# Gates by Tanh with the halves folded into later factors, and the channel norm traced at high priority, in a hybrid decoder layer

## The chip, the cores and the metric

The kernel runs on one core of a Trainium2 chip. A core has a matrix engine (TensorE; PE for its matmuls and PEld for its weight loads in the profile), a vector engine (DVE), an activation engine for pointwise functions (ACT), a general engine (GpSimd; POOL), and a synchronisation engine (SP), which here issues most of the transfers between the chip's memory and the core's own memory (SBUF). TensorE writes its products into a separate memory, PSUM, which DVE and ACT read. Each engine works through its own queue in order and waits at semaphores for the others. The metric is the device time of one execution, in microseconds (us); less is better.

## What is computed

One layer: an input projection `proj = rmsnorm(x) @ w_in` is cut into the inputs of three head groups. Their outputs, side by side, go through `w_out` and are added to `x`, and a last norm follows. All is in 32-bit floating point; x is 512 tokens of 2048 features.

```python
u = cv_a * jax.nn.sigmoid(cv_b)                       # 4 groups of 128 channels
u = causal_depthwise_conv(u, conv_w[l], conv_b[l])    # 31 taps
u = jax.nn.silu(layernorm(u, conv_ln_g[l], conv_ln_b[l]))   # over 512 channels
y_conv = (u @ w_conv_pw[l]) * jax.nn.silu(cv_gate)

y_fox = fox_attention(fq, fk, fv, logf)               # 8 heads, causal, with a forget bias
y_fox = y_fox * jax.nn.silu(fox_gate)

y_mem = memory_attention(mq, mk, mv)                  # 4 heads, into 256 memory tokens
y_mem = y_mem * jax.nn.silu(mem_gate)

x = x + jnp.concatenate([y_conv, y_fox, y_mem], axis=-1) @ w_out[l]
return rmsnorm(x, final_g)
```

## The kernel before

**Operands.** TensorE gets each 32-bit operand as two parts, a rounded high part and the rest. `split` (L90) makes them: a copy on ACT (L93, or L96 with a scale), then a subtraction on DVE (L94, or L97 with a scale). A product is three matmuls: high by high, high by low, low by high. `operand` (L127) does this for a piece of weights that SP has loaded into one of six `raw` buffers; the pair of parts goes into one of three `wb` buffers.

**Projections in pairs.** `pair` (L525) projects two blocks of 128 features at once by seven products in place of eight, with sums of the tokens' quarters made beforehand (`s1` to `s4`). Each product is 24 matmuls at L549. Between products DVE subtracts weight pieces from one another (L511, `raw<-raw,raw`, 128 x 1024) and adds partial results (L508), and ACT copies partial results out of PSUM (L522, L559). A pair hands on its first block as two halves in PSUM (`x1`, `x2`) and its second as a tile `col` in SBUF.

**What runs between.** The list `work` (L971) gives the order of the pairs. Per head of the forgetting attention there is one pair for query and key, one for gate and value (F_G, F_V), and behind heads 0, 2 and 4 one for a group of conv channels. What has to be done with a pair's result is put into `slots`, a queue of small pieces; after each product one piece is taken (`beside`, L513), and from `bg` one convolution tap (L383). `gate_values` (L858) is such a piece: it computes the gate by Silu on ACT out of PSUM in two halves (L862) and transposes the values. `probs` (L888) makes the scores on TensorE, adds the bias and takes the extremum on DVE (L896), the exponential on ACT (L900), the reciprocal of its sum on DVE (L901) and the scaling on ACT (L902). `attend` (L904) transposes the probabilities, multiplies by the values and then by the gate on DVE (L928; L931 for the last head), and POOL's queue stores the result (L929).

**The convolution.** `conv_channels` (L365) computes sigmoid of the gate block (L371) into `up`, multiplies by the other block (L375) and queues 31 taps: the first as an affine on ACT with the bias (L378), the others on DVE (L383). The taps' weights `cwt` come out of a transpose in PSUM (L307). The four results go to the chip's memory and are read back for the norm.

**The channel norm and its product.** The piece `norm` (L953) stands in `slots` behind the attention of head 6. It closes the attention's pool of tiles, loads the four channel groups (`open_norm`, L688, on SP through `queued`), subtracts the mean (`centre`, L696) and divides by the deviation (`normalise`, L706). The sums over channels are matmuls by a constant matrix (L684, L685). The reciprocal root is an exponential of a logarithm on ACT (L717, L718) and one Newton step on DVE (L719 to L721). During this the pairs of the conv gates run (`after_gates`, L725; Silu at L729 and L730), then the pair of query and key of head 7. In the middle of that pair's program order stands `project_conv` (L734): Silu of the normed channels on ACT (L739), the split into `csh` and `csl`, and 48 matmuls of 512 columns.

**Order.** The code is a trace: the program gives dependences and a first order, and a planner at build time sets each engine's final order by simulated times, with earlier traced work first among what is ready. `tc.high_priority()` puts the instructions traced inside it ahead of the others that are ready. `queued` keeps its SP transfers in the order of the program; `issue_after` keeps an instruction behind another on the same engine. Where two functions that follow one another on ACT don't share a table, the build puts a table load (ACT_TABLE_LOAD) ahead of the second.

Of the kernel before, what the change touches and what calls it, by code (L numbers as in the profile page):

```python
# [13 lines left out]
AF = mybir.ActivationFunctionType  # L14
ALU = mybir.AluOpType
# [32 lines left out]
def hybrid_layer_kernel(  # L48
# [18 lines left out]
    nc = tc.nc  # L67
# [12 lines left out]
    def nm(s):  # L80
        uid[0] += 1
        return f"{s}_{uid[0]}"
# [100 lines left out]
    with tc.tile_pool(name="start", bufs=1) as st:  # L183
# [119 lines left out]
        for c in range(CW // P):  # L303
            nc.tensor.transpose(
                pt[:, c * TAPS : (c + 1) * TAPS], cwr[:, c * P : (c + 1) * P], ident[:TAPS, :TAPS]
            )
        nc.vector.tensor_copy(cwt.rearrange("p c j -> p (c j)"), pt)  # L307

    conv_b_c = lambda c: cols[:, 2 * KT + c : 2 * KT + c + 1]
    ln_g_c = lambda c: cols[:, 2 * KT + 4 + c : 2 * KT + 5 + c]  # L310
# [51 lines left out]
    def halves(t):  # L362
        return [t[:, :M], t[:, M:]]

    def conv_channels(c, xs, gate):  # L365

        background(len(bg))
        up = cp.tile([P, PAD + S], F32, tag="up", name=nm("up"))
        acc = cp.tile([P, S], F32, tag="acc", name=nm("acc"))
        nc.gpsimd.memset(up[:, 0:PAD], 0.0)  # L370
        nc.scalar.activation(up[:, PAD:], gate, AF.Sigmoid)  # L371
        w = S // len(xs)
        for i, x_ in enumerate(xs):
            u = up[:, PAD + i * w : PAD + (i + 1) * w]
            nc.vector.tensor_tensor(u, x_, u, ALU.mult)  # L375

        def first():
            nc.scalar.activation(  # L378
                acc, up[:, 0:S], AF.Identity, scale=cwt[:, c, 0:1], bias=conv_b_c(c)
            )  # L380

        def tap(j):
            return lambda: nc.vector.scalar_tensor_tensor(  # L383
                acc, up[:, j : j + S], cwt[:, c, j : j + 1], acc, ALU.mult, ALU.add
            )

        bg.append(first)
        bg.extend(tap(j) for j in range(1, TAPS))
        bg.append(lambda: nc.gpsimd.dma_start(out=accd[c], in_=acc))
# [298 lines left out]
    def open_norm():  # L688
        lp = ln["pool"] = lnpool.enter_context(tc.tile_pool(name="ln", bufs=1, reuse_waits="tile"))
        background(len(bg))  # L690
        acc = ln["acc"] = [lp.tile([P, S], F32, name=f"la{c}") for c in range(NC)]
        for c in range(NC):
            queued(acc[c], accd[c])
        ln["gates"] = [lp.tile([P, S], F32, name=f"lg{c}") for c in range(NC)]

    def centre():  # L696
        acc = ln["acc"]
        total = spare()
        nc.vector.tensor_tensor(total, acc[0], acc[1], ALU.add)
        for c in range(2, NC):  # L700
            nc.vector.tensor_tensor(total, total, acc[c], ALU.add)
        mu = over_channels(total)
        for c in range(NC):
            nc.vector.tensor_tensor(acc[c], acc[c], mu, ALU.subtract)
# [153 lines left out]
    def gate_values(xs, col):  # L858
        fx = fox["pool"]
        gate = fx.tile([P, S], F32, tag="fgate", name=nm("fgate"), bufs=2)  # L860
        for x_, g in zip(xs, halves(gate)):
            nc.scalar.activation(g, x_, AF.Silu)  # L862
        vp = at()
        for j in range(NT):
            sl = slice(j * P, (j + 1) * P)
            nc.tensor.transpose(vp[:, sl], col[:, sl], ident)
        v = tuple(fx.tile([P, NT, P], F32R, tag=t, name=nm(t)) for t in ("vh", "vl"))
        split(*v, vp.rearrange("p (j d) -> p j d", d=P))
        return gate, v
# [34 lines left out]
    def attend(h, gv, pr):  # L904

        pth, ptl = fox["h"], fox["l"]

        def transposes(j):
            n = S - j * P
            tp = at((P, n))  # L910
            for i in range(j, NT):
                nc.tensor.transpose(  # L912
                    tp[:, (i - j) * P : (i - j + 1) * P], pr[i][:, j * P : (j + 1) * P], ident
                )
            w = max(n, M)
            split(pth[j][:, w - n :], ptl[j][:, w - n :], tp)

        def values():
            gate, (vh, vl) = gv
            ov = at()  # L920
            for j in range(NT):
                w = max(S - j * P, M)
                mm3(
                    ov[:, S - w :], (vh[:, j, :], vl[:, j, :]), (pth[j], ptl[j]),
                    j == 0, j == NT - 1,
                )
            if h < NH - 1:
                nc.vector.tensor_tensor(gate, ov, gate, ALU.mult)  # L928
                nc.gpsimd.dma_start(out=yd[4 + h], in_=gate)  # L929
            else:  # L930
                nc.vector.tensor_tensor(last["y"], ov, gate, ALU.mult)  # L931

        return [lambda: (transposes(0), transposes(1)), lambda: (transposes(2), transposes(3)), values]

# [11 lines left out]
    def after_gv(h):  # L946
        def f(xs, col):
            gv = []
            slots.append(lambda: gv.extend(gate_values(xs, col)))
            slots.extend(attend(h, gv, pr.pop(h)))  # L950
            if h == NH - 2:

                def norm():  # L953
                    fpool.close()
                    open_norm()
                    centre()
                    normalise()

                slots.append(norm)

        return f
# [243 lines left out]
```

## Time and profile before

| | us |
|---|---|
| median of three runs | 861.43 |
| lowest and highest of the three | 858.65, 862.3 |
| the profiled execution, its own time | 862.33 |
| its span, first to last instruction | 860.4 |
| its mean granted TensorE clock | 0.990 of full |

In the profile's lines L12 stands for line 12 of the kernel. A group of instructions is given as line, engine, operation, written tile `<-` read tiles, shapes and count, then its busy time in us, the mean duration of one in ns, and the idle time of its engine just before it with what ended that idle time. The chain that ended last is followed back from the last instruction to what released each step. Matmuls overlap one another, so a busy time of PE says that matmuls are under way, and not that they follow at the best rate.

### The profile page before, as it was taken

Reading aid. Unit: us, or ns where it says so; the run is one execution under the profiler, and the core shown is the slowest. Engines: PE = TensorE matmul, PEld = TensorE weight load, DVE = VectorE, ACT = ScalarE, POOL = GpSimd, SP = SyncE. Lnnn points to the kernel's source line nnn. Section 1 sums busy time; section 2 is a strip of 40 time slices with the busy share of each in tenths; the row PEclk is TensorE's granted clock in tenths of the full one; section 3 lists DMA queues with packets and bytes.
Section 4 is the critical chain, followed back from the end, with each engine's and each line's share of the span. In section 5 each row is a group of like instructions: output and inputs, shape, how many; then the busy total and the mean of one; then the engine's idle time right before and its main releaser. Section 6 shows DMA issues by size and latency. Waiting matters only on the chain.

```text
span 860.4 us, 15416 instructions
## 1 busy us (share of the span) xinstructions
PE 830.4 (97%) x6212; PEld 790.2 (92%) x6212; DVE 713.3 (83%) x1031; ACT 508.4 (59%) x806; POOL 59.3 (7%) x86
## 2 busy tenths in 40 slices
PE   7999999999989999999999999999979999999996
PEld 6898899999989999999999999989979988998995
DVE  4589999999779899899899897987885977876964
ACT  4875466556786675655756566575583952443523
POOL 1021000000012010011000020200000000000001
PEclk9999999999999999999999999999999999999999
DMA  8973303443434333543234433444443718361415
GB/s 311 329 220 78 85 16 101 123 111 104 117 99 105 102 102 85 149 107 94 74 109 122 106 105 98 124 110 129 129 123 103 253 45 298 98 199 47 149 48 195
DMA packets 144262, 109.76 MB, mean 128 GB/s; under 512 B 4060, under 2 KB 127032, under 8 KB 143552
## 3 DMA queue, kind: packets, MB, share of 16 engines
q1 hardware_dynamic: 142272, 103.57, 41.8%
q0 software_dynamic: 1920, 5.23, 1.7%
q8 instruction: 48, 0.79, 0.4%
q14 instruction: 22, 0.18, 0.1%
HBM read 99.55 MB, written 9.22 MB: 126 GB/s over the span
## 4 chain that ended last, share of the span: by engine, by line
PE 81%; DVE 8%; ACT 7%; issue 3%; DMA 1%; SPq 0%; POOL 0%; POOLq 0%; ACTq 0%; DVEq 0%
PE pj L549 44%; PE pj L1106 8%; PE pj L104 5%; PE pj L105 5%; PE pj L106 5%; PE at L104 3%; PE at L106 3%; PE at L105 3%; ACT wb L93 2%; DVE raw L511 2%; DVE wb L94 2%; DVE acc L383 1%; PE at L912 1%; ACT L900 1%; DMA raw<-in_w_mem_kv_dram 1%
## 5 line engine op out<-in xcount | busy, mean ns | idle before, releaser
L94 DVE TENSOR_TENSOR wb<-raw,wb 128x1024 fp32r<-128x1024 f32 x232 | 283.4, 1224 | 65.5 <-ACT wb L93 64.9
L93 ACT CAST wb<-raw 128x1024 fp32r<-128x1024 f32 x232 | 241.0, 1050 | 157.7 <-PE pj L549 44.2
L549 PE MATMUL pj<-hh,wb 128*128 128x256 f32 x1536 | 289.6, 283 | 5.7 <-ACT wb L93 4.2
L549 PEld LDWEIGHTS pj<-hh,wb 128*128 128x128 f32 x1536 | 243.4, 191 | 7.8 <-issue 4.2
L549 PE MATMUL pj<-hl,wb 128*128 128x256 f32 x768 | 216.6, 282 | 0.0
L549 PEld LDWEIGHTS pj<-hl,wb 128*128 128x128 f32 x768 | 146.6, 191 | 0.8
L511 DVE TENSOR_TENSOR raw<-raw,raw 128x1024 f32<-128x1024 f32 x112 | 136.5, 1219 | 0.4
L383 DVE SCALAR_TENSOR_TENSOR acc<-up,cwt,acc 128x512 f32<-128x512 f32 x120 | 89.4, 745 | 0.0
L1106 PE MATMUL pj<-wb,rh 128*128 128x256 f32 x672 | 80.1, 279 | 0.7 <-DVE sst L1160 0.4
L1106 PEld LDWEIGHTS pj<-wb,rh 128*128 128x128 f32 x672 | 79.4, 188 | 1.4 <-DVE res L1032 1.1
L549 PE MATMUL pj<-s1h,wb 128*128 128x256 f32 x384 | 74.2, 284 | 4.2 <-DVE wb L94 4.2
L549 PE MATMUL pj<-s2h,wb 128*128 128x256 f32 x384 | 73.5, 280 | 0.0
L549 PE MATMUL pj<-s0h,wb 128*128 128x256 f32 x384 | 71.3, 279 | 1.9 <-ACT wb L93 1.9
L549 PEld LDWEIGHTS pj<-s1h,wb 128*128 128x128 f32 x384 | 60.1, 188 | 5.3 <-DVE wb L94 5.2
L549 PEld LDWEIGHTS pj<-s0h,wb 128*128 128x128 f32 x384 | 60.4, 188 | 2.3 <-ACT wb L93 2.1
L549 PEld LDWEIGHTS pj<-s2h,wb 128*128 128x128 f32 x384 | 60.8, 188 | 0.0
L549 PE MATMUL pj<-s2l,wb 128*128 128x256 f32 x192 | 53.6, 279 | 0.0
L549 PE MATMUL pj<-s0l,wb 128*128 128x256 f32 x192 | 53.5, 279 | 0.0
L549 PE MATMUL pj<-s1l,wb 128*128 128x256 f32 x192 | 53.4, 278 | 0.0
L881 POOL TENSOR_SCALAR_AFFINE_SELECT b<-b 128x128 f32<-128x128 f32 x32 | 29.9, 942 | 237.7 <-ACT b L880 237.3
L549 PEld LDWEIGHTS pj<-s2l,wb 128*128 128x128 f32 x192 | 36.1, 188 | 0.1
L549 PEld LDWEIGHTS pj<-s1l,wb 128*128 128x128 f32 x192 | 36.1, 188 | 0.0
(301 smaller groups left out, 1391.2 us busy)
## 6 DMA issues: line engine op xcount, KB each, us to landing
raw<-in_w_in_dram SPq DMA_DIRECT2D x104, 512.0 KB, 4.2
raw<-in_w_out_dram SPq DMA_DIRECT2D x32, 512.0 KB, 5.1
raw<-in_w_mem_kv_dram SPq DMA_DIRECT2D x12, 512.0 KB, 7.6
xr<-in_x_dram SPq DMA_DIRECT2D x4, 1024.0 KB, 8.2
res<-in_x_dram SPq DMA_DIRECT2D x8, 512.0 KB, 6.8
out_dram<-res SPq DMA_DIRECT2D x16, 256.0 KB, 2.8
rs<-yd SPq DMA_DIRECT2D x15, 256.0 KB, 4.4
mr<-in_mem_dram SPq DMA_DIRECT2D x8, 256.0 KB, 7.9
```

The source lines that it names most:

```text
L93: ins = nc.scalar.copy(hi, src)
L94: low = nc.vector.tensor_tensor(lo, src, hi.bitcast(F32), ALU.subtract)
L104: nc.tensor.matmul(o, ah, bh, start=start, stop=False)
L105: nc.tensor.matmul(o, ah, bl, start=False, stop=False)
L106: nc.tensor.matmul(o, al, bh, start=False, stop=stop)
L383: return lambda: nc.vector.scalar_tensor_tensor(acc, up[:, j : j + S], cwt[:, c, j : j + 1], acc, ALU.mult, ALU.add)
L511: nc.vector.tensor_tensor(o, p, q, ALU.subtract)
L549: mm = nc.tensor.matmul(o, p[:, k, :], q, start=start and k == 0 and i == 0, stop=k == HK - 1 and i == 2, skip_group_check=True,)
L881: nc.gpsimd.affine_select(out=b[:, sl], in_=b[:, sl], pattern=[[-1, P]], compare_op=ALU.is_ge, fill=-MASKED, base=0, channel_multiplier=1,)
L900: nc.scalar.activation(b, b, AF.Exp, bias=ng, scale=-1.0, accum_out=sm)
L912: nc.tensor.transpose(tp[:, (i - j) * P : (i - j + 1) * P], pr[i][:, j * P : (j + 1) * P], ident)
L1106: nc.tensor.matmul(o[:, m, :], p, q[:, k, :], start=start and k + m + i == 0, stop=k == HK - 1 and i == 2, skip_group_check=True,)
```

## The change

The heads' gate is computed as x (1 + tanh(x/2)), which is twice Silu(x): a Tanh on ACT with a scale of 0.5, then a multiply-add on DVE that reads the projected gate out of PSUM again. The missing half is a factor in the multiply by the attention's values. In the convolution, sigmoid(z) becomes 1 + tanh(z/2), twice the sigmoid, and the multiply by the other block becomes a multiply-add; the half goes into the taps' weights, where they are copied out of PSUM. The memory heads' gates, the conv gates and the Silu behind the norm stay as they are. The three parts of the norm are traced at high priority.

```diff
-        nc.vector.tensor_copy(cwt.rearrange("p c j -> p (c j)"), pt)
+        nc.vector.tensor_scalar(cwt.rearrange("p c j -> p (c j)"), pt, 0.5, None, ALU.mult)
...
-        nc.scalar.activation(up[:, PAD:], gate, AF.Sigmoid)
+        nc.scalar.activation(up[:, PAD:], gate, AF.Tanh, scale=0.5)
         w = S // len(xs)
         for i, x_ in enumerate(xs):
             u = up[:, PAD + i * w : PAD + (i + 1) * w]
-            nc.vector.tensor_tensor(u, x_, u, ALU.mult)
+            nc.vector.scalar_tensor_tensor(u, u, 1.0, x_, ALU.add, ALU.mult)
...
         for x_, g in zip(xs, halves(gate)):
-            nc.scalar.activation(g, x_, AF.Silu)
+            nc.scalar.activation(g, x_, AF.Tanh, scale=0.5)
+            nc.vector.scalar_tensor_tensor(g, g, 1.0, x_, ALU.add, ALU.mult)
...
             if h < NH - 1:
-                nc.vector.tensor_tensor(gate, ov, gate, ALU.mult)
+                nc.vector.scalar_tensor_tensor(gate, ov, 0.5, gate, ALU.mult, ALU.mult)
                 nc.gpsimd.dma_start(out=yd[4 + h], in_=gate)
             else:
-                nc.vector.tensor_tensor(last["y"], ov, gate, ALU.mult)
+                nc.vector.scalar_tensor_tensor(last["y"], ov, 0.5, gate, ALU.mult, ALU.mult)
...
                 def norm():
                     fpool.close()
-                    open_norm()
-                    centre()
-                    normalise()
+                    with tc.high_priority():
+                        open_norm()
+                        centre()
+                        normalise()
```

## The prediction

> **What bounds the kernel now.** I read the page first, for the engine that is full and the chain that ended last; then the groups of instructions, for what the change touches; then busy time by stretch, to find where the full engine stands still; last the chain and the order of time at one such place.
>
> ```profile
> span 860.4 us, 15416 instructions
> ...
> PE 830.4 (97%) x6212; PEld 790.2 (92%) x6212; DVE 713.3 (83%) x1031; ACT 508.4 (59%) x806; POOL 59.3 (7%) x86
> ...
> PE 81%; DVE 8%; ACT 7%; issue 3%; DMA 1%; SPq 0%; POOL 0%; POOLq 0%; ACTq 0%; DVEq 0%
> ```
>
> TensorE is the bound: it is busy 97% of the span and holds 81% of the chain. The change takes nothing from it, so a gain can only come out of the 30 us (860.4 - 830.4) in which it stands still, and out of time at a lowered clock. An activation engine (ACT) that is busy 59% is no bound by itself; what matters is the places where the chain leaves TensorE. The change stands in two stages, the heads' attention (about 233 to 600 us) and the channel norm with the convolution's last product (600 to 660 us). There, by stretch (length, busy time of PE, PEld, DVE, ACT, POOL, each with its count, granted clock, DMA share, GB/s):
>
> ```profile
> 341.00:400.00 59.00, 59.00 (x507) 58.82 (x506) 53.26 (x71) 34.54 (x53) 6.74 (x7) 1.00 0.45 121
> 255.00:259.00 4.00, 1.84 (x13) 1.44 (x12) 4.00 (x9) 3.43 (x9) 0.00 (x0) 1.00 0.07 9
> 259.90:263.30 3.40, 3.40 (x18) 3.40 (x17) 2.84 (x3) 0.98 (x2) 0.00 (x0) 0.50 0.29 86
> 289.00:292.00 3.00, 2.06 (x18) 1.86 (x17) 2.54 (x7) 2.97 (x6) 0.00 (x0) 1.00 0.00 0
> ...
> 415.00:418.00 3.00, 1.09 (x10) 0.92 (x9) 3.00 (x5) 1.65 (x3) 0.00 (x0) 1.00 0.41 100
> ...
> 526.50:529.50 3.00, 1.09 (x10) 0.92 (x9) 3.00 (x5) 1.65 (x3) 0.00 (x0) 1.00 0.41 96
> 529.60:533.00 3.40, 3.40 (x18) 3.40 (x17) 3.40 (x4) 1.26 (x1) 0.00 (x0) 0.50 0.20 59
> 560.00:563.00 3.00, 2.06 (x18) 1.86 (x17) 2.70 (x7) 2.97 (x6) 0.00 (x0) 1.00 0.00 0
> 576.00:578.50 2.50, 1.32 (x12) 1.15 (x11) 2.50 (x4) 0.95 (x2) 0.00 (x0) 1.00 0.35 74
> 637.50:642.50 5.00, 0.87 (x8) 0.67 (x6) 5.00 (x9) 4.07 (x5) 0.00 (x0) 0.97 0.66 197
> 642.50:649.00 6.50, 6.16 (x25) 5.77 (x26) 4.44 (x5) 2.23 (x4) 0.00 (x0) 0.50 0.00 0
> ```
>
> Between the stalls the stage runs without a hole (59.00 of 59.00 in 341 to 400). The stalls are of three kinds. Four, at 255, 415, 526 and 576, idle TensorE 2.16, 1.91, 1.91 and 1.18 us: 7.16 us. Four alike, of which 289 and 560 are shown, idle it 0.94 us each: 3.76 us. The norm idles it 4.13 us at 637.5 and 0.34 us after. Behind three of them the granted clock is 0.50: 3.4 us each at 259.9 and 529.6, 6.16 us of busy time at 642.5. Half speed costs half of that time: 1.7, 1.7 and 3.1 us.
>
> The Trainium skill ("TensorE: Matmul & The Clock Gate", Part 1) lowers the clock after an idle window of about 3.4 us. By that rule the idle times of 2.16 and 1.91 us would leave it alone; the 0.50 rows behind them say otherwise, so this trace disagrees and the rows are used.
>
> What makes a stall of the first kind, in the chain and in the order of time on DVE (start, length, what, and in brackets the idle time before it with its releaser):
>
> ```profile
> 408.90 1.28 ACT L862
> ...
> 410.60 1.28 ACT L900
> ...
> 411.89 1.41 ACT b L900 x4
> ...
> 415.42 1.23 DVE raw L511
> ...
> 416.73 1.06 ACT wb L93
> ...
> 412.63 0.16 DVE L901 RECIPROCAL sm<-sm 128x1 f32<-128x1 f32 x1 [2.39 <-ACT b L900]
> 289.45 0.29 DVE L896 CUSTOM_DVE_ANT_0 b<-at,b 128x128 f32<-128x128 f32 x1 [2.53 <-PE at L106]
> ```
>
> Two table loads of 1.28 us stand in ACT's queue between the gate (L862) and the softmax's exponential (L900). DVE waits 2.39 us for the exponential's sum; behind that wait stands the subtraction L511, behind it the cast L93, and behind that TensorE. The second kind has no load in it: DVE's queue stands at L896 for scores that TensorE has not reached, with an operand's low half (L94) behind it.
>
> **The change, part by part.** The times of the operations (count, then busy us, mean ns, idle before):
>
> ```profile
> L900 ACT ACT_TABLE_LOAD x13 | 16.7, 1283 | 0.2
> L862 ACT ACT_TABLE_LOAD x13 | 16.7, 1283 | 0.2
> L371 ACT ACT_TABLE_LOAD x4 | 5.1, 1283 | 0.1
> L862 ACT ACTIVATE fgate<-pj 128x256 f32<-128x256 f32 x16 | 6.2, 385 | 13.7 <-PE pj L549 13.6
> L97 DVE SCALAR_TENSOR_TENSOR fq<-pj,fq 128x256 fp32r<-128x256 f32 x16 | 6.5, 417 | 2.2 <-ACT fq L96 2.2
> L375 DVE TENSOR_TENSOR up<-pj,up 128x256 f32<-128x256 f32 (+1 forms) x7 | 3.2, 462 | 3.4 <-ACT up L371 2.0 <-PE pj L549 1.5
> ```
>
> *Loads.* No row shows Tanh, so the loads that go are bounded from 0 to all those at L862 (13), twelve of the thirteen at L900 (one stands behind the Silu of L739 and stays) and two at L371 (of its four, the one behind the memory gates' Silu stays; the first I leave). The conv gates' Silu (L729), which today finds its table loaded, gets one. Net 13 + 12 + 2 - 1 = 26 loads, 26 x 1.283 = 33.4 us of ACT. I take all: the copies, identities and squares of L93, L880 and L709 run between the exponentials and gates without a load of their own, so one table does serve several functions, and only Exp against Silu or Sigmoid alternates here. Nearly all of the 33.4 us lies beside TensorE's work (ACT is busy 34.54 of 59.00 us in a stretch without a hole). On the path are the first kind's stalls: 7.16 us idle and 1.7 + 1.7 us of half clock, 10.6 us.
>
> The Trainium skill ("ScalarE: Activation LUTs", Table sets: the hidden batching unit) lists exp and tanh in one set; no run here shows it. Its section What ACT_TABLE_LOAD costs adds a drain of about 1.38 us to each load. By it the 26 loads would be worth some 69 us of ACT, an estimate from that page; in this trace the exponential starts 0.01 us behind the load (410.60 + 1.28 to 411.89), so 1.283 us is used.
>
> *The multiply that Silu did.* Each half gate gets a multiply-add on DVE that reads PSUM: 16 more, 128 x 256, with two tensors and a constant. L97 is that form: 417 ns, 16 x 0.417 = 6.7 us. Tanh itself I cost as the Silu it replaces (385 ns). In 341 to 400 DVE is busy 53.26 of 59.00 us; 0.83 us per head (a head lasts about 46 us, 233 to 600 for eight) hides in the rest. For the four long stalls: DVE has 2.39 us of wait to give back at 412.63 and gets 0.42 us more, so 1.97 us are left against an idle time of 1.91. They close, barely; I leave the one at 576 (1.18 us) open as the price of a new order of instructions and take 10.6 - 1.2 = 9.4 us. What is late next is DVE itself.
>
> *A wait added.* The multiply waits for ACT's Tanh, which waits for TensorE's product. ACT waited 13.6 us at L862 for products; the multiply stands in DVE's queue, and operand halves (L94) and subtractions (L511) stand behind it, with TensorE waiting for those. L97 behind L96 is the same pattern in the query pairs: DVE waited 2.2 us in all over 16. So from 0 to about one stall of the second kind per head, 8 x 0.94 = 7.5 us. I take 1.0, near L97's row. PSUM is released later by such a wait too; the buffers are next needed more than a product away, and I cost that at nothing.
>
> *The rest.* The factor 0.5 in L307, L928 and L931 rides in an instruction that exists, and the conv's multiply (L375) becomes the form of L97: within 50 ns each, some 20 instructions, under 1 us beside TensorE. The first table at L371 (87 us) has no stall behind it: nothing.
>
> *The norm.* The whole chain is traced at high priority: four loads on SP, DVE's sums, subtractions and Newton steps, ACT's squares, Ln, Exp, and four matmuls.
>
> ```profile
> L109 SPq DMA_DIRECT2D la<-accd x4: 370/378/533, 597.6 to 599.2; - x4
> L699 DVE TENSOR_TENSOR spare<-la,la x1: 686/686/686, 604.5 to 604.5; 128x512 f32<-128x512 f32 x1
> 604.00:643.00 39.00, 10.71 (x16) 4.92 (x8) 0.99 0.43 123
> L704 DVE TENSOR_TENSOR la<-la,at x4: 679/680/680, 614.5 to 616.3; 128x512 f32<-128x512 f32 x4
> 639.47 1.28 ACT L739
> ...
> 600.00:638.00 38.00, 38.00 (x325) 37.78 (x325) 32.16 (x38) 24.36 (x35) 0.00 (x0) 1.00 0.48 142
> 405.01 2.80 PE pj L549 x24
> L94 DVE TENSOR_TENSOR wb<-raw,wb 128x1024 fp32r<-128x1024 f32 x232 | 283.4, 1224 | 65.5 <-ACT wb L93 64.9
> L511 DVE TENSOR_TENSOR raw<-raw,raw 128x1024 f32<-128x1024 f32 x112 | 136.5, 1219 | 0.4
> L508 DVE TENSOR_TENSOR col<-pj,p 128x256 f32<-128x256 f32 x24 | 10.0, 417 | 0.2 <-PE pj L549 0.2
> ```
>
> The loads leave SP at 597.6, as soon as the attention's tiles are free, so priority can't start the chain much before its first sum at 604.5. It ends at 640.8 where L739 begins: 36 us. Its own DVE work is 10.71 us on `spare` (the 39 us row is that tile's instructions alone, DVE then ACT) and 4 x 0.68 = 2.7 us at L704: 13.4 us. A pair of projections takes seven products of 2.80 us, 19.6 us of TensorE, and costs DVE 7 x 1.224 + 4 x 1.219 + 2 x 0.417 = 14.3 us: 5.3 us in 19.6 are free. DVE was idle 38.00 - 32.16 = 5.8 us in 600 to 638, and 3.4 us of the norm (L721 and the four products of L723, 0.68 each as at L704) came after. So the norm fits before TensorE needs it, but with only 2.4 us to spare; done sooner, it pushes operand halves back. Gain from 0 (the stall only moves) to 4.13 + 0.34 + 3.1 = 7.6 us. I take 5.0: the half clock and most of the stall go, 2.6 us come back as small holes in 605 to 640.
>
> **The sum** on the profiled execution's own time, 862.33 us (its span is 860.4): 862.3 - 9.4 - 5.0 + 1.0 = 848.9 us. The three runs shown have a median of 861.43, 0.9 us lower, so the forecast is 848.0 us.
>
> **The rivals**, each on the same footing (less 0.9).
>
> B. *The norm's stall moves.* Packed into less time its 13.4 us of DVE starve the operands, and TensorE loses between 605 and 640 what it gains at 637. For it: 2.4 us to spare. Against: three operand buffers carry TensorE over short delays. 862.3 - 9.4 + 1.0 - 0.9 = 853.0.
>
> C and D start from one row of the list of waits (total us, times, longest):
>
> ```profile
> ACT fgate L862 <- PE pj L549: 13.6, 6, 3.1
> ```
>
> C. *DVE's new wait takes the place of the loads.* There are six places where ACT stood at L862; at each the multiply holds DVE and TensorE loses what it loses now at a long stall, 1.91 us: 11.5 in place of 1.0. 862.3 - 9.4 - 5.0 + 11.5 - 0.9 = 858.5.
>
> D, on the other side. *The same wait, long enough to drop the clock.*
>
> The longest of the six waits is 3.1 us. At 526 a stall of 1.91 us brought 1.7 us of half clock: 3.6 us each, 21.7 for six: 862.3 - 14.4 + 21.7 - 0.9 = 868.7. It is slower than before from 14.4 / 6 = 2.4 us a place, by over 0.5% from 3.1. For it: operands queue behind L896 in the same way now. Against: L97, in the same pattern, waits 2.2 us in all.
>
> E. *The loads stay.* If the table that Tanh brings lacks Exp, nothing goes at L862 and L900: 862.3 - 5.0 + 1.0 - 0.9 = 857.4.
>
> ```profile
> L717 ACT ACT_TABLE_LOAD  x1: 1283/1283/1283, 631.4 to 631.4; - x1
> L718 ACT ACT_TABLE_LOAD  x1: 1283/1283/1283, 634.3 to 634.3; - x1
> ```
>
> For it: Ln and Exp, one after the other in the norm, each load a table. The Trainium skill ("ScalarE: Activation LUTs", Table sets: the hidden batching unit) knows a set that holds both, and would have one load there; the trace has two, so a shared set is not always the one taken.
>
> **How the numbers follow.** Chances: A (forecast, 843 to 852) 0.48, B 0.20, C 0.14, D 0.11, E 0.07. Within 0.5% of 861.43, 857.1 to 865.7, is about what a measurement of this kernel can tell from no change. A and B are faster: 0.68. C and E lie within: 0.21. D: 0.11. The range starts where all stalls close, the 3.76 us of the second kind too: 861.4 - 10.6 - 7.6 - 3.8 = 839.4, rounded to 840, and reaches over B, E and C to 860; D and a little of C are left out.
>
> **What would show it.** Right: no ACT_TABLE_LOAD at the gate's line, 26 fewer in all; ACT some 33 us less busy, DVE some 7 us more; stretches of 59 us with PE at 59.00 where 415 and 526 lie; no 0.50 clock between 100 and 850 us; the norm's last product before TensorE's last projection. Wrong: DVE idle before the gate's multiply with its releaser ACT, and PE waiting for L94 right behind (C, D); PE holes between the norm's sums (B); loads at the gate (E). A new order of instructions elsewhere, which the trace of before can't show, would make the sum wrong without any of these.

## The result and the profile after

The kernel after takes 849.97 us (median of 4 runs, 849.09 to 851.48), the kernel before in the same session 860.04 us (858.25 to 862.3). The ratio is 0.9883, with a 95% interval of 0.9852 to 0.9915. The profiled execution took 849.81 us, 12.5 us less than the profiled execution of before (862.33).

The page of the kernel after: its span, and the busy time of each engine (share of the span, instructions). From here on the lines of the kernel after are numbered as in that kernel: the gate's Tanh is L864, its multiply-add L865, the exponential L903, the pair products L550.

```profile
span 848.0 us, 15403 instructions
...
PE 824.6 (97%) x6212; PEld 785.7 (93%) x6212; DVE 717.3 (85%) x1047; ACT 472.6 (56%) x778; POOL 59.2 (7%) x86
```

ACT is 35.8 us less busy (508.4 to 472.6) and has 28 instructions fewer; they are all table loads (43 before, 15 after). DVE has 16 instructions and 4.0 us more. Three groups of instructions of the kernel after (line, engine, operation, count, then busy us, mean ns, idle before and its releaser):

```profile
L865 DVE SCALAR_TENSOR_TENSOR fgate<-fgate,pj 128x256 f32<-128x256 f32 x16 | 6.6, 412 | 1.6 <-ACT fgate L864 1.6
L864 ACT ACTIVATE fgate<-pj 128x256 f32<-128x256 f32 x16 | 6.1, 380 | 15.4 <-PE pj L550 15.4
L903 ACT ACT_TABLE_LOAD x2 | 2.6, 1283 | 0.0
```

No load stands at the gate's line any more, and two of thirteen are left at the exponential's. The multiply-add costs 412 ns and waits 1.6 us in all for its Tanh.

Where the time went is seen best by laying the same work side by side. Busy time by stretch (length, PE, PEld, DVE, ACT, POOL, granted clock, DMA share, GB/s), first the attention of the heads and the 100 us behind it in the kernel before:

```profile
233.00:600.00 367.00, 355.59 (x2952) 351.38 (x2951) 319.07 (x454) 234.06 (x374) 34.68 (x41) 0.99 0.39 105
600.00:700.00 100.00, 95.53 (x669) 89.52 (x669) 82.64 (x128) 67.52 (x115) 3.69 (x8) 0.97 0.44 139
```

and then in the kernel after, with single stretches of it below:

```profile
233.00:587.50 354.50, 350.73 (x2952) 347.84 (x2951) 322.95 (x469) 201.69 (x348) 34.70 (x41) 1.00 0.40 108
587.50:687.50 100.00, 95.47 (x671) 89.29 (x670) 83.81 (x132) 67.23 (x115) 3.62 (x8) 0.97 0.46 140
...
235.00:285.00 50.00, 50.00 (x422) 49.60 (x421) 44.31 (x69) 32.49 (x59) 6.23 (x10) 1.00 0.39 107
285.00:288.00 3.00, 2.06 (x17) 1.86 (x17) 2.97 (x7) 1.86 (x6) 0.00 (x0) 1.00 0.00 0
333.00:440.00 107.00, 107.00 (x908) 106.47 (x908) 98.31 (x139) 59.85 (x102) 12.30 (x12) 1.00 0.42 112
443.00:549.00 106.00, 106.00 (x900) 105.47 (x899) 97.77 (x137) 59.28 (x101) 12.28 (x12) 1.00 0.42 113
552.00:625.50 73.50, 73.50 (x622) 73.01 (x622) 61.98 (x79) 44.29 (x68) 1.08 (x2) 1.00 0.48 132
625.50:630.60 5.10, 0.62 (x7) 0.42 (x5) 5.10 (x9) 4.45 (x6) 0.00 (x0) 0.84 0.56 171
629.00:635.80 6.80, 5.24 (x20) 4.86 (x21) 5.66 (x7) 3.45 (x6) 0.00 (x0) 0.50 0.11 42
```

The same 2952 matmuls of the attention take 354.5 us in place of 367.0: 12.5 us, which is the whole difference. TensorE's idle time there falls from 11.41 us (367.00 - 355.59) to 3.77 us (354.50 - 350.73), that is by 7.64 us, and its busy time by 4.86 us. 3.4 us of these are the two stretches at half clock (3.4 us each), which are gone; the other 1.4 us are taken up further down. The four long stalls are gone: TensorE runs without a hole over 50, 107, 106 and 73.5 us. The 3.77 us that are left are the four stalls of the second kind (0.94 us each), one of which is the row at 285.

The norm's 100 us haven't changed at all: 4.47 us idle before, 4.53 after, a clock of 0.97 in both. TensorE still stands still for 4.48 us at 625.5 (5.10 - 0.62), and 6.8 us of half clock follow.

What became of a long stall, in the order of time (start, length, engine, line, operation, idle before it) in the kernel after, ACT first and DVE second:

```profile
402.78 1.05 ACT L93 CAST wb<-raw 128x1024 fp32r<-128x1024 f32 x1 [1.98 <-PE pj L550]
403.74 0.38 ACT L864 ACTIVATE fgate<-pj 128x256 f32<-128x256 f32 x1
404.01 0.61 ACT L903 ACTIVATE b<-b,ng 128x384 f32<-128x384 f32 x1
```

```profile
405.11 0.41 DVE L865 SCALAR_TENSOR_TENSOR fgate<-fgate,pj 128x256 f32<-128x256 f32 x1
405.44 0.15 DVE L904 RECIPROCAL sm<-sm 128x1 f32<-128x1 f32 x1
```

Gate and exponential follow one another without a load; before, 2.57 us of loads stood there. DVE's reciprocal, which waited 2.39 us for the exponential, now waits for nothing, although the multiply-add stands right before it.

### The profile page after: what moved, and what is told of

Its sections match the earlier page's. It is cut to its first block, busy times and chain, and to the rows that moved or that the text cites. A ratio compares the mean times of both kernels' runs of the same rounds, so it can differ in the third digit from the quotient of the medians.

```text
span 848.0 us, 15403 instructions
## 1 busy us (share of the span) xinstructions
PE 824.6 (97%) x6212; PEld 785.7 (93%) x6212; DVE 717.3 (85%) x1047; ACT 472.6 (56%) x778; POOL 59.2 (7%) x86
## 5 line engine op out<-in xcount | busy, mean ns | idle before, releaser
L94 DVE TENSOR_TENSOR wb<-raw,wb 128x1024 fp32r<-128x1024 f32 x232 | 282.9, 1222 | 59.5 <-ACT wb L93 59.1
L550 PE MATMUL pj<-hh,wb 128*128 128x256 f32 x1536 | 286.0, 281 | 0.5 <-ACT wb L93 0.4
L550 PEld LDWEIGHTS pj<-hh,wb 128*128 128x128 f32 x1536 | 240.7, 189 | 1.7 <-ACT wb L93 0.9
L550 PE MATMUL pj<-hl,wb 128*128 128x256 f32 x768 | 214.6, 279 | 0.0
L550 PEld LDWEIGHTS pj<-hl,wb 128*128 128x128 f32 x768 | 145.0, 189 | 0.8
L512 DVE TENSOR_TENSOR raw<-raw,raw 128x1024 f32<-128x1024 f32 x112 | 136.2, 1216 | 0.4
L550 PE MATMUL pj<-s1h,wb 128*128 128x256 f32 x384 | 74.1, 284 | 3.8 <-DVE wb L94 3.8
L550 PE MATMUL pj<-s2h,wb 128*128 128x256 f32 x384 | 73.8, 280 | 0.0
L550 PE MATMUL pj<-s0h,wb 128*128 128x256 f32 x384 | 71.0, 278 | 0.0
L550 PEld LDWEIGHTS pj<-s1h,wb 128*128 128x128 f32 x384 | 60.1, 188 | 4.7 <-DVE wb L94 4.6
L550 PEld LDWEIGHTS pj<-s2h,wb 128*128 128x128 f32 x384 | 60.8, 188 | 0.1
L550 PEld LDWEIGHTS pj<-s0h,wb 128*128 128x128 f32 x384 | 60.2, 188 | 0.0
L550 PE MATMUL pj<-s2l,wb 128*128 128x256 f32 x192 | 53.6, 279 | 0.0
L550 PE MATMUL pj<-s0l,wb 128*128 128x256 f32 x192 | 53.5, 279 | 0.0
L550 PE MATMUL pj<-s1l,wb 128*128 128x256 f32 x192 | 53.4, 278 | 0.0
L550 PEld LDWEIGHTS pj<-s2l,wb 128*128 128x128 f32 x192 | 36.1, 188 | 0.1
L550 PEld LDWEIGHTS pj<-s1l,wb 128*128 128x128 f32 x192 | 36.1, 188 | 0.0
```

The lines of the kernel that those rows point to most:

```text
L94: low = nc.vector.tensor_tensor(lo, src, hi.bitcast(F32), ALU.subtract)
L512: nc.vector.tensor_tensor(o, p, q, ALU.subtract)
L550: mm = nc.tensor.matmul(o, p[:, k, :], q, start=start and k == 0 and i == 0, stop=k == HK - 1 and i == 2, skip_group_check=True,)
```

## The experiments

A time is the median of a kernel's runs; a ratio is to the kernel before, run in the same session on the same chip, with a 95% interval (its median there was 862.0 us beside the kernels without the priority and with gates, convolution or loads alone; 861.78 beside the lower priority, the memory gates, the norm without loads and the later product; 861.32 beside the other three). The diffs are against the kernel after, except where it is said otherwise.

### Without the high priority

```diff
-                    with tc.high_priority():
+                    if True:
```

> The changed kernel with the norm traced at plain priority. Theory 1 (the priority moves no instruction; the norm's stall is in both traces alike): 850.0 us, as the changed kernel, within 2 us, with the stall of about 4.7 us ahead of the conv product and the half clock behind it. Rival (the term of 5.0 us for the norm is in the measured gain, and the loads brought less): 855 us.

850.82 us, ratio 0.9866 (0.985 to 0.9882). The stall before the norm's products, in busy time by stretch:

```profile
625.50:630.60 5.10, 0.63 (x6) 0.43 (x4) 5.10 (x8) 4.56 (x6) 0.00 (x0) 0.89 0.54 164
```

It is the same stall at the same place (4.47 us against 4.48). The program says why: with and without the priority it holds the same instructions in the same order on all five engines. And the kernel before with the priority alone has, too, the order of the kernel before. The priority moves nothing. So 849.97 and 850.82 us are medians of one and the same order of instructions, and the 0.85 us between them show how far medians from two sessions can lie apart.

### The norm at a lower priority

That the priority moves nothing could mean that the planner doesn't heed priorities, or that the norm was first already. So the norm was put behind other work instead:

```diff
-                    with tc.high_priority():
-                        open_norm()
-                        centre()
-                        normalise()
+                    tc.cur_priority += 400
+                    open_norm()
+                    centre()
+                    normalise()
+                    tc.cur_priority -= 400
```

> The kernel after, with the norm traced at a LOWER priority (400 steps later for the planner) in place of a higher one; nothing else differs. Theory 1 (the norm already had the first place among the work that is ready, so raising its priority moved nothing, and the planner does obey priorities): the norm's instructions now fall behind operand halves on DVE, its last product comes later, TensorE's stall of 4.75 us before the last pair of products grows to 6 us or more, and the time is 852 to 860 us. Theory 2 (the engines' work at the norm has slack, its place in the queue hardly matters): 848.5 to 851.5 us with the stall as in the kernel after.

856.12 us, ratio 0.9941 (0.9923 to 0.9959), as theory 1 expects. In busy time by stretch TensorE now stands still for 12.00 us:

```profile
624.00:636.50 12.50, 0.50 (x4) 0.30 (x3) 8.77 (x13) 8.42 (x10) 0.00 (x0) 0.61 0.15 46
626.80:640.50 13.70, 4.19 (x16) 3.82 (x17) 8.05 (x11) 7.70 (x10) 0.00 (x0) 0.50 0.01 3
```

The planner does obey priorities, and being first is worth 5.3 us to the norm (856.12 - 850.82). It had that before the change; the likely reason, read from the program and not tested, is that its code is traced ahead of the work that it competes with.

### The heads' gates alone

The kernel before with Tanh, the multiply-add and the folded half in the heads' gates; the convolution keeps its sigmoid. Against the kernel before:

```diff
-            nc.scalar.activation(g, x_, AF.Silu)
+            nc.scalar.activation(g, x_, AF.Tanh, scale=0.5)
+            nc.vector.scalar_tensor_tensor(g, g, 1.0, x_, ALU.add, ALU.mult)
```

> Tanh and the multiply-add in the heads' gates alone; the convolution keeps its sigmoid, the norm its plain priority. Theory 1 (the four long stalls are the loads at the gates and the exponentials): 850.7 us, all of the gain but the stall of 0.64 us that stood behind the sigmoid's load at 231 us. Rival (the sigmoid's loads delay the heads too): over 853 us.

849.04 us, ratio 0.9852 (0.9837 to 0.9866). All four long stalls are gone. One short stall of before is left, and isn't in the kernel after:

```profile
235.50:237.50 2.00, 1.52 (x14) 1.32 (x13) 1.83 (x3) 1.77 (x2) 0.00 (x0) 1.00 0.37 139
```

It lies behind the load at the convolution's sigmoid (L372, at 230.4 us).

### The convolution alone

Against the kernel before, with the half in the taps' weights as well:

```diff
-        nc.scalar.activation(up[:, PAD:], gate, AF.Sigmoid)
+        nc.scalar.activation(up[:, PAD:], gate, AF.Tanh, scale=0.5)
...
-            nc.vector.tensor_tensor(u, x_, u, ALU.mult)
+            nc.vector.scalar_tensor_tensor(u, u, 1.0, x_, ALU.add, ALU.mult)
```

> Tanh in the convolution alone; the gates keep Silu, the norm its plain priority. Theory 1: 859.4 us, 0.6 us under the kernel before, with the four long stalls where they were. Rival: under 857 us.

860.7 us, ratio 0.9986 (0.9976 to 0.9995): some 1.2 us. Five loads go, the stall at 236 with them, and the long stalls stay. With the starts of the matmuls, whose order is the same, laid beside those of before, the stall at 236 is worth 0.57 us. Another 1.27 us of the profiled execution come at the norm, where the same 4.48 us of idle time are followed by 3.4 us at half clock in place of 6.8. Busy time by stretch around two of the long stalls:

```profile
255.00:259.00 4.00, 1.85 (x13) 1.43 (x12) 4.00 (x7) 3.44 (x7) 0.00 (x0) 1.00 0.12 19
259.00:265.00 6.00, 6.00 (x52) 5.89 (x51) 4.88 (x6) 4.34 (x7) 0.00 (x0) 1.00 0.27 75
414.06:417.47 3.41, 1.50 (x13) 1.43 (x13) 3.41 (x5) 2.43 (x3) 0.00 (x0) 1.00 0.55 154
...
417.00:421.00 4.00, 4.00 (x24) 4.00 (x23) 2.99 (x4) 1.23 (x3) 0.00 (x0) 0.57 0.00 0
```

Here the stall at 255 (2.15 us idle) leaves the clock alone, and the one at 414 (1.91 us) lowers it; in the kernel before it was the other way round. The section on the hardware comes back to it.

### The loads alone

The kernel before with Tanh in place of Silu at the gates, and no multiply by the gate's input. Nothing is added, so the order of the work on TensorE, DVE, GpSimd and SyncE stays as before, and ACT only loses 21 table loads.

```diff
-            nc.scalar.activation(g, x_, AF.Silu)
+            nc.scalar.activation(g, x_, AF.Tanh, scale=0.5)
```

> The kernel before with Tanh in place of Silu at the heads' gates and nothing else: the multiply by the gate's input is left out, so no instruction is added on the vector engine and only table loads go. Theory 1 (loads alone make the gain, the added multiply costs next to nothing): 850.7 us, within 1 us of the gates alone. Rival (the 16 multiplies on the vector engine cost the 7.5 us of my upper bound or a part of it): 2 to 7 us less than the gates alone, 844 to 849 us.

849.65 us, ratio 0.9857 (0.9842 to 0.9872). Its attention in busy time by stretch:

```profile
233.00:600.00 367.00, 362.75 (x3055) 359.74 (x3054) 328.00 (x464) 215.14 (x366) 34.51 (x41) 1.00 0.40 109
```

The idle time is 4.25 us (the four short stalls and the one at 237). The loads alone give the gain: 862.0 - 849.65 = 12.35 us for 21 x 1.283 = 26.9 us of ACT. And the 16 multiply-adds cost nothing that shows: with them it is 849.04 us, and from the first load at the exponential to the load at the conv gates' Silu it is 341.4 us without them and 341.6 us with them.

### Tanh in the memory heads' gates, too

In the kernel after, loads are left at the memory heads' gates (L589, 4) and at their exponentials (L604, 3). On the kernel without the priority:

```diff
-        nc.scalar.activation(gate, src, AF.Silu)
+        nc.scalar.activation(gate, src, AF.Tanh, scale=0.5)
+        nc.vector.scalar_tensor_tensor(gate, gate, 1.0, src, ALU.add, ALU.mult)
...
-            nc.vector.tensor_tensor(gate[0], ov[0], gate[0], ALU.mult)
+            nc.vector.scalar_tensor_tensor(gate[0], ov[0], 0.5, gate[0], ALU.mult, ALU.mult)
```

> The kernel after without the priority, and with the memory heads' gates, too, by Tanh and a multiply-add on DVE in place of Silu. Theory 1 (a load is worth something only where TensorE waits behind it; in the memory stage TensorE stands still for only 0.57 us and DVE has little time to spare): no gain from it, 850 to 853 us. Theory 2 (each load costs time wherever it stands): the loads at the memory gates go and 1.28 us comes off for each of the four or more: 846 us or less.

849.5 us, ratio 0.9861 (0.9836 to 0.9886), which its interval can't tell from 850.82 (0.9866). ACT is 8.1 us less busy (464.5 of 472.6); the time isn't. The memory stage, first in the kernel after and then here:

```profile
133.00:233.00 100.00, 99.52 (x830) 97.81 (x829) 91.44 (x128) 64.33 (x115) 3.39 (x7) 1.00 0.42 113
```

```profile
133.00:233.00 100.00, 99.73 (x836) 98.28 (x836) 93.81 (x132) 57.51 (x109) 3.41 (x7) 1.00 0.42 111
```

TensorE had 0.48 us to win in these 100 us and won 0.21. Seven loads go (three at L589, three at L604, the first at the heads' exponential), each as long as those at the heads' gates, and there is no gain, because TensorE didn't wait behind them: from the first load at L589 to that of the conv gates it is 464.1 us without the edit and 464.3 us with it. (The expectation of theory 1, 850 us or more, was half a microsecond too high.)

### What holds the norm: its loads

The norm's stall is the largest that is left, so four kernels take its chain apart. All are without the priority and are compared with 850.82 us (ratio 0.985 to 0.9882), which is from another session. The intervals of the ratios overlap with that one for every kernel of this and the next three sections but the one with both edits, so the stalls in the traces have to carry the argument together with the times. First the three loads (the third is at the Silu of the normed channels, L740), by a norm that leaves the reciprocal root out:

```diff
-        nc.scalar.activation(rs, ve, AF.Ln)
-        nc.scalar.activation(rs, rs, AF.Exp, scale=-0.5)
+        nc.scalar.activation(rs, ve, AF.Identity)
+        nc.scalar.activation(rs, rs, AF.Identity, scale=-0.5)
```

> The kernel after without the priority, and with the norm's Ln and Exp replaced by Identity (the reciprocal root of the norm is left out): three table loads of 1.28 us go from ACT, at the Ln, the Exp and the memory gate's Silu behind the norm; every other instruction and their order stay. Theory 1 (the three loads stand in the norm's chain behind one another and nothing covers them): the stall of 4.75 us shrinks by up to 3.85 us and the half clock behind it with it, 844 to 847.5 us. Theory 2 (DVE's sums and TensorE's products set the end, and the loads lie beside them): 849 to 851.5 us, stall above 4 us.

847.99 us, ratio 0.9843 (0.9819 to 0.9866): between the two theories. Busy time by stretch:

```profile
625.20:629.00 3.80, 0.57 (x6) 0.37 (x5) 3.80 (x8) 3.15 (x5) 0.00 (x0) 1.00 0.76 209
629.00:632.40 3.40, 3.40 (x12) 3.02 (x13) 3.40 (x5) 1.87 (x3) 0.00 (x0) 0.51 0.00 0
```

Three loads are 3.85 us; the stall loses 1.25 us (4.48 to 3.23), about one load's length. So the larger part of the loads lies beside other work here. The half clock behind it lasts 3.4 us in place of 6.8. In the kernel after TensorE is busy for 5.24 us of those 6.8, which costs it 2.6 us, here for 3.40, which costs 1.7: 0.9 us. Together that is 2.2 us, where the medians say 2.83 and the spans of the profiled executions 2.5 (848.3 - 845.8). Whether the shorter stall is what saved the half clock stays open: the kernels with the gates alone and with the convolution alone have 3.4 us of half clock, too, behind a stall of full length (4.47 and 4.48 us).

### What holds the norm: its Newton step

The order of time on DVE in the kernel after, from the Exp's result to the products by the root (L724):

```profile
623.95 0.69 DVE L720 TENSOR_TENSOR spare<-spare,spare 128x512 f32<-128x512 f32 x1 [0.72 <-ACT spare L719]
624.55 0.42 DVE L509 TENSOR_TENSOR col<-pj,u 128x256 f32<-128x256 f32 x1
624.89 0.68 DVE L721 SCALAR_TENSOR_TENSOR spare<-spare,spare 128x512 f32<-128x512 f32 x1
625.49 1.22 DVE L94 TENSOR_TENSOR wb<-raw,wb 128x1024 fp32r<-128x1024 f32 x1
626.62 0.68 DVE L722 SCALAR_TENSOR_TENSOR spare<-spare,spare 128x512 f32<-128x512 f32 x1
627.23 0.41 DVE L509 TENSOR_TENSOR col<-pj,p 128x256 f32<-128x256 f32 x1
627.56 2.48 DVE L724 TENSOR_TENSOR la<-la,spare 128x512 f32<-128x512 f32 x4
```

The same two ends in the kernel before:

```profile
636.24 0.69 DVE L719 TENSOR_TENSOR spare<-spare,spare 128x512 f32<-128x512 f32 x1 [0.72 <-ACT spare L718]
...
639.85 2.48 DVE L723 TENSOR_TENSOR la<-la,spare 128x512 f32<-128x512 f32 x4
```

In both it is 3.61 us, to the hundredth: the chain is the same, 12.29 us earlier. Three instructions of 0.68 us take those 3.61 us, because an operand's low half (L94) and two sums (L509) stand between them. This kernel leaves the Newton step out:

```diff
-        nc.vector.tensor_tensor(ve, ve, rs, ALU.mult)
-        nc.vector.scalar_tensor_tensor(ve, ve, -0.5, rs, ALU.mult, ALU.mult)
-        nc.vector.scalar_tensor_tensor(rs, ve, 1.5, rs, ALU.add, ALU.mult)
```

> The kernel after without the priority, and without the norm's Newton step (three instructions on DVE, 0.68 us each, that refine the reciprocal root; the root stays as Ln and Exp give it). Theory 1 (DVE is the engine that is short before the stall: what comes back is the time of the three, 2.0 us, and with a stall of some 2.6 us one of the two 3.4 us windows of half clock, 1.7 us): 846.5 to 848 us. Theory 2 (the norm's chain is late by its latency: in the kernel after 3.65 us pass between the end of the Exp and the first product by the root, since operand halves stand between the three; all of it goes, the stall is 1 us and the half clock goes whole): 842.5 to 845 us. Neither (no change at the stall): 850 to 851 us.

847.6 us, ratio 0.9852 (0.982 to 0.9883), the time of theory 1, but not by its reason. In busy time by stretch, and in the order of time on DVE and on ACT (here L721 is the product, L737 the Silu):

```profile
626.00:629.70 3.70, 0.80 (x6) 0.56 (x5) 3.01 (x6) 3.69 (x6) 0.00 (x0) 1.00 0.37 101
630.20:633.60 3.40, 3.40 (x10) 2.62 (x9) 2.73 (x3) 1.29 (x2) 0.00 (x0) 0.51 0.33 117
```

```profile
624.36 2.50 DVE L721 TENSOR_TENSOR la<-la,spare 128x512 f32<-128x512 f32 x4 [0.72 <-ACT spare L719]
```

```profile
624.23 1.03 ACT L93 CAST wb<-raw 128x1024 fp32r<-128x1024 f32 x1
625.28 1.28 ACT L737 ACT_TABLE_LOAD   x1
626.58 2.23 ACT L737 ACTIVATE la<-la,cols 128x512 f32<-128x512 f32 x3
```

The products do follow the Exp at once, 3.61 us sooner, as theory 2 had it. But the stall shrinks only by 1.58 us (4.48 to 2.90): the first product, done after 0.68 us, at 625.04, has its Silu start only at 626.58, behind a cast and the Silu's table load on ACT. In the kernel after that load (627.18 to 628.46 us) ends only 0.2 us behind the first product (628.24 us); with the step gone it is what is late next.

### What holds the norm: when it is needed

Here the norm stays whole, and the convolution's last product, which needs it, comes two TensorE products (5.6 us) later:

```diff
-            before[1](*next(before[0]))
+            done = next(before[0])
+            if fa == F_G + (NH - 1) * P:
+                project_conv()
+                lnpool.close()
+                open_fox()
+            before[1](*done)
...
-            if fa == F_Q + (NH - 1) * P:
-                project_conv()
-                lnpool.close()
-                open_fox()
```

> The kernel after without the priority, and with the convolution's last product (which needs the whole norm) put two TensorE products of 2.8 us later in the order of the work; nothing else differs. Theory 1 (the norm's chain is late by its latency: some 5.5 us more of other TensorE work cover it): the stall of 4.75 us and the half clock behind it (6.83 us at 0.50, 3.4 us lost) go, 842 to 845 us. Theory 2 (DVE is short of time there, so that the products put ahead are late by as much as the norm): the stall moves or splits up, 848.5 to 852 us.

849.43 us, ratio 0.9863 (0.9837 to 0.9888). The 5.6 us of cover bring 1.4 by the medians, which the intervals don't tell from nothing. Busy time by stretch:

```profile
628.00:630.00 2.00, 0.77 (x8) 0.59 (x6) 2.00 (x4) 0.00 (x0) 0.00 (x0) 1.00 0.42 111
632.50:636.00 3.50, 0.55 (x6) 0.35 (x4) 2.07 (x4) 3.47 (x6) 0.00 (x0) 0.97 0.47 147
```

The stall is in two pieces, 1.23 and 2.95 us. Why the cover was lost, in the order of time on DVE and on ACT:

```profile
623.83 0.69 DVE L720 TENSOR_TENSOR spare<-spare,spare 128x512 f32<-128x512 f32 x1 [0.72 <-ACT spare L719]
...
630.85 1.29 DVE L724 TENSOR_TENSOR la<-la,spare 128x512 f32<-128x512 f32 x2
```

```profile
631.47 1.06 ACT L93 CAST wb<-raw 128x1024 fp32r<-128x1024 f32 x1 [4.44 <-DMA raw<-in_w_conv_pw_dram]
632.55 1.28 ACT L740 ACT_TABLE_LOAD   x1
633.84 1.52 ACT L740 ACTIVATE la<-la,cols 128x512 f32<-128x512 f32 x2
```

From L720 to the products it is 7.02 us now, not 3.61: the two TensorE products put ahead bring their subtractions (L512) and low halves (L94), and these queue between the norm's instructions. That takes 3.4 of the 5.6 us. Then ACT stands 4.44 us at a cast whose weights haven't landed, with the Silu behind it. DVE is short, as theory 2 says, but the late weights count as well; the runs don't part the two.

### Both together, and one root in place of Ln and Exp

The later product without the Newton step (both diffs above):

> As in the kernel without the Newton step, with the convolution's last product two TensorE products later as well. Theory 1 (DVE is short; later work on TensorE needs operands from the same DVE): the idle time falls by the 2.0 us of the three instructions against the kernel that has it later with the step (849.4 us, stalls 1.4 and 3.1 us), and the last half clock may go: 845.5 to 847.5 us. Theory 2 (latency: two products more cover the rest): no stall over 0.5 us between 600 and 640 us and no half clock there, 842 to 844 us.

843.84 us, ratio 0.9811 (0.9783 to 0.9839), the fastest of all: 1.9% below the kernel before, 6.1 us below the kernel after. It leaves out the refinement of the root. Busy time by stretch:

```profile
628.00:630.00 2.00, 1.30 (x11) 1.13 (x10) 2.00 (x3) 2.00 (x5) 0.00 (x0) 1.00 0.03 10
```

A stall of 0.70 us is left, a little more than theory 2 allowed, and the clock stays at 1.00. Apart the two edits give 1.4 and 3.2 us, together 7.0 us (by the spans of the profiled executions 0.7, 2.3 and 6.1 us): either alone leaves a stall behind which the clock falls.

The later product with the Newton step, and one activation for the root:

```diff
-        nc.scalar.activation(rs, ve, AF.Ln)
-        nc.scalar.activation(rs, rs, AF.Exp, scale=-0.5)
+        nc.scalar.activation(rs, ve, AF.Abs_reciprocal_sqrt)
```

> As in the kernel with the convolution's last product two products later, and the norm's Ln and Exp replaced by one activation that gives the reciprocal root (Abs_reciprocal_sqrt): one ACT pass of 0.63 us and one table load of 1.28 us fewer in the norm, DVE's work the same. Theory 1 (DVE is short; ACT's time lies beside): 848.5 to 850 us, as with Ln and Exp (849.4). Theory 2 (ACT's share of the chain counts, 1.9 us): stalls of 1.4 and 3.1 us shrink by 1.9 us, 846 to 847.5 us.

846.87 us, ratio 0.9842 (0.9814 to 0.9869), as theory 2 says: ACT's 1.9 us in the chain count. TensorE is idle for 2.23 us, and the clock stays:

```profile
628.50:631.50 3.00, 0.77 (x7) 0.60 (x6) 3.00 (x6) 2.18 (x4) 0.00 (x0) 1.00 0.46 163
```

This kernel leaves nothing of the computation out and is 3.1 us faster than the kernel after.

## Why the prediction was right, and where it was wrong

The forecast was 848.0 us, 13.4 us off the 861.43 it started from, with a range of 840 to 860; 849.97 was measured, and on the profiled execution the sum of 848.9 stands against 849.81. The total is close because misses cancel: the loads brought 3.1 us more than taken and the wait cost 1.0 us less, the norm 5.0 us less. So a part of the closeness is luck. By the terms of the sum:

| term | taken | shown by the runs |
|---|---|---|
| loads | -9.4 | -12.5 (stage, profiled), -12.35 (the loads alone) |
| norm at high priority | -5.0 | 0 |
| the multiply-add's wait | +1.0 | 0 within the intervals (849.04 with, 849.65 without; 0.2 us in the stage) |

**The norm's step failed.** It took 5.0 of 7.6 us because "the norm fits before TensorE needs it, but with only 2.4 us to spare". Two things in that step were wrong. It took for granted that a high priority brings the norm's work forward, and only asked whether DVE has room for it; the norm was first already, no instruction moved, and the gain was 0. And it counted DVE's time over 36 us as if the norm could use it in any order. The norm is a chain: in the kernel after, at 623 to 631, each of its steps waits for the one before it on another engine, or behind other work in a queue. The rows of before showed it, with DVE busy 5.00 of 5.00 us and ACT 4.07 through the stall, and loads of 1.28 us at L717, L718 and L739 in the chain. A gain of 0 was named as an end of the range, for a stall that only moves; that the priority may do nothing had no chance of its own. A rival "the loads go, the norm stays" would have read 862.3 - 9.4 + 1.0 - 0.9 = 853.0, the figure of B by another mechanism. The measured time lies 2.0 us from the forecast and 3.0 us from that figure, so the number alone hardly tells them apart; the runs do.

**The loads: the mechanism was right, the size was not.** The kernel with the loads alone shows that they and nothing else closed the four long stalls. Too little was taken in three places. The stall at 576 (1.18 us), left open as the price of a new order, closed. A fifth stall, 0.48 us at 236 behind the load of the convolution's sigmoid, wasn't in the sum; that load, which was said to stay behind the memory gates' Silu, went. And the stage's busy time fell by 4.86 us where 3.4 us of half clock were counted. These last 1.4 us don't show as idle time. With the starts of the matmuls of before laid beside those of the kernel with the loads alone, which have the same order, the four long stalls delay TensorE by 2.7, 2.15, 2.15 and 1.4 us, 8.4 in place of the 7.16 us that are idle, and 0.6 us more are lost at 305.5 to 315 us, where matmuls follow more slowly behind the loads at 298.9 and 300.6 us without a hole.

**The count of loads** was 28, not 26: all four at the convolution's gate went rather than two, one more at L427, and one less at the exponential. That one table serves Exp and Tanh was taken from the copies and squares that run between; it holds, and rival E falls: from the first head's Exp to the convolution's gates, 248 to 589 us, the kernel after has no load. The Trainium skill ("ScalarE: Activation LUTs", Table sets: the hidden batching unit) lists exp and tanh in one set, and the trace agrees.

**C and D** (DVE's new wait takes the stalls' place) fell: L865 waits 1.6 us in all, as L97 in the same pattern did, and TensorE stands still behind none of it. The reason lies in the row of 13.6 us at L862 from which both started: ACT waits there for TensorE, but by the time DVE reaches L865 in its own queue the Tanh is done (at the place shown above, 403.74 + 0.38 against 405.11).

**The second kind** of stall was left out of the sum and is unchanged, 0.94 us four times: rightly so.

**The signs to look for** came as foretold for the gate's line, ACT's time (35.8 us less where some 33 were said) and the long stretches without a hole. DVE rose by 4.0 us where some 7 were said: the new instructions are 6.6 us, and others came out a little shorter (the 232 low halves at L94 282.9 us in place of 283.4). The signs "no 0.50 clock between 100 and 850 us" and "the norm's last product before TensorE's last projection" did not come.

## What to carry to other kernels

A table load costs what TensorE waits behind it, and no more: 21 loads at the heads' gates and exponentials were worth 12.35 us, seven others where TensorE hardly stands still nothing that the intervals show. Before counting on a priority, see whether the work isn't first already, and whether it is late by its queue or by the chain of its own waits; a chain is helped by fewer steps and by a later need, best by both at once. Where a stall lowers the clock, a microsecond off it can pay more than its length, but the clock behind it can also change with nothing but where the stall falls.

## What the runs showed of the hardware

Half clock came in units of some 3.4 us: 3.4 us behind 2.16 and 1.91 us idle in the kernel before, 3.4 us behind 3.23 and 2.90 us (no loads, no Newton step in the norm), and 13.7 us at and behind 12.00 us. The same length of idle time does not always bring the same. In the kernel before the stall at 255 lowered the clock and the one at 415 didn't; with the convolution alone it was the other way round; 2.23 us idle left the clock at 1.00 in the kernel with one root. Behind the 4.47 or 4.48 us at the norm it was 6.8 us in five kernels (before, after, without the priority, the loads alone, the memory gates) and 3.4 us in two (the gates alone, the convolution alone).

The traces' own record of the granted clock says why. Within a trace it changes only at whole multiples of 3.413 us from one another; in the kernel before the first two falls of the stages above, at 259.90 and 529.56 us, lie 79 of them apart. So the clock is set by windows that run on their own. Busy time by stretch in two such windows of the kernel before:

```profile
413.50:416.92 3.42, 2.38 (x21) 2.17 (x19) 2.99 (x5) 2.07 (x4) 0.00 (x0) 1.00 0.07 10
416.92:420.33 3.41, 2.54 (x22) 2.58 (x23) 3.41 (x5) 2.41 (x3) 0.00 (x0) 1.00 0.51 144
```

The stall at 415 falls into both, 1.04 and 0.87 us of it, and the clock stays; with the convolution alone it lies whole in one (the row 414.06:417.47 above, 1.91 us idle), and half clock follows. The 2.23 us of the kernel with one root fall into two windows as well, 0.69 and 1.54 us of them. In all 13 traces, from 60 us on, every such window at full clock with 1.91 us idle or more is followed by half clock, and none with 1.85 us or less but one (1.67 us, at 256.5 in the kernel before). So a stall of about 2 us counts or not by where it falls in these windows. The Trainium skill ("TensorE: Matmul & The Clock Gate", Part 1: The HAM clock gate) has a free-running window of 3413 ns, which agrees with the record; that it takes a whole idle window to lower the clock does not agree with 1.91 us.

The table that Silu brings serves Tanh as well: between the memory gates' last load (219 us) and the first Exp (248 us) the kernel after has no load, though the convolution's Tanh (232 us) stands between. The prediction had a load stay there; it was worth the 0.48 us at 236.
